# Hybrid attention layer, one core: the first projection pass's weight casts, its two scale-and-shift sums and the late normalisations in another order

## The chip, the cores and the metric

The kernel runs on one core of a Trainium2 chip. The metric is the device time of one execution in microseconds (us). Before the change it is 689.31 us, the median of 3 runs (689.22 to 689.42).

The core has five engines with a queue each: PE (TensorE, matrix products), ACT (ScalarE), DVE (VectorE), POOL (GpSimd) and SP, which here only issues transfers (DMAs). An engine takes its instructions in order, and where one needs another engine's result it waits on a semaphore. PE writes its results to PSUM; ACT and DVE read them there ("evacuate" them).

## What is computed

One residual layer over 1024 rows x 1024 columns, cut to the part that matters here:

```
u = layer_norm(x) * (1 + scale) + shift        # scale, shift = silu(c) @ w_ada + b_ada
h = u @ w_in                                   # q, k, v, g of two groups of 8 heads
y = [forgetting attention | stick-breaking attention] * silu(g)
out = layer_norm(1.19 * x + gate * (y @ w_out)) * ln_g + ln_b
```

Everything is float32 in and out. The products are made at nearly that precision out of two rounded parts: an operand a becomes `hi`, its value rounded to a shorter format, and `lo`, the rounded remainder a - hi. A product then is three: hi x hi, lo x hi and hi x lo. So for every operand somebody has to make a *cast* (hi) and a *remainder* (lo).

## The kernel before: the first pass

The change lies within the first 55 us, the first pass over the projection. It works on rows 0 to 511 (four tiles x_0 to x_3 of 128 rows) and makes five products at once (`ALL`, the names `st_q`, `st_k`, `st_g`, `st_q`, `st_k` in the profile): q, k and g of head pair 0, q and k of pair 1. The width of 1024 is cut into eight blocks, `kb` = 0 to 7, and the loop at L672 takes them one after the other. For block kb+1, while PE multiplies block kb:

- SP loads the weights: `wss` (w_ada's two slices, for scale and shift, `load_ss`, L152), `raws` (the slice of w_in for four of the five products, `load_w4`, L574; one load brings blocks 4 and 5 together, another 6 and 7).
- DVE sums scale and shift out of `wss` (`mod_terms`, L233: two instructions L230 for each block, part 0 and part 1, each followed by a short read-out into `modc`).
- PE transposes the four x tiles' 128 columns into the PSUM tile `xT_early` (`u_turn`, L239, L242). There is one such tile for all blocks from 2 on, so the transposes of a block wait until the last reader of the block before is through.
- ACT makes `uh` of it, the cast of u (L248), and writes the unrounded u back into `xT_early` (L249); together that is `u_round`.
- DVE makes `ul`, the remainder of u, out of both (`u_rest`, L260, L261). It is the last reader of `xT_early`.
- ACT makes the cast of the weights and POOL their remainder (`start_split`, L575 to L599; the names are `whi_stk`/`wlo_stk` for blocks 0 to 2 and `hw` from block 3 on, in pairs of blocks: one `hw` holds 3 and 4, the next 5 and 6, the last 7).

PE's order is written out by hand (`manual_schedule`) and so is SP's. In a block it is: four products with the weights' casts (hi), four with their remainders (lo), the four transposes of block kb+1, the fifth product's two, then the five products with `ul` (`start_steps`, L601). The order of ACT, DVE and POOL is set by a scheduler; `with after(i)` tells it that an instruction goes behind i, and `in_turn` (L223) chains the sums and `ul` among themselves in the order written.

After block 7 the first value tiles follow (`v_first`, L781: rows of v for pairs 0 and 1, `v_tile` L346): tile 0 into one half of the PSUM tile `st_late`, tile 1 into `v`, tile 2 into the other half of `st_late`, tile 3. Each has four evacuations, in turn ACT (L360) and DVE (L361), twice. Then `late_round` (L773) makes u of rows 512 to 1023 in the same way, and for that x_4 to x_7 have to be normalised (`norm_stats` L208, `norm_x` L213): x_4 and x_5 by ACT (L218), x_6 and x_7 by DVE (L217, `NORM_ON`), behind their statistics (L197, L198, L189 on DVE, L191 and L192 on POOL).

At the very start PE is kept busy with products whose result nobody reads (`busy`, L174; `WARM`, L75): four before anything else, one behind the transposes of x_0 and one behind those of x_1 (L639).

Of the kernel before, what the change touches and what calls it, by code (L numbers as in the profile page):

```python
# [8 lines left out]
F32 = mybir.dt.float32  # L9
F32R = mybir.dt.float32r  # L10
AF = mybir.ActivationFunctionType
ALU = mybir.AluOpType

P = 128
SEQ = 1024
D = 1024
NB = 8
# [10 lines left out]
def tile_hybrid_layer(  # L28
# [17 lines left out]
    nc = tc.nc  # L46
# [21 lines left out]
    def t_tile(name):  # L68
        return ps.tile([P, 512], F32, tag="T", bufs=2, name=name)
# [2 lines left out]
        return ps.tile([P, 2, 512], F32, tag="S", bufs=1, name=name)  # L72

    RING = 5
    WARM = (4, 1, 1, 0, 0)  # L75
    NORM_ON = {6: nc.vector, 7: nc.vector}
    FLOG = 4
    FROW = 8
# [4 lines left out]
    def after(*instructions):  # L83
        stack = ExitStack()
        for i in instructions:
            stack.enter_context(tc.issue_after(i.ins))
        return stack


    ident = cp.tile([P, P], F32, tag="ident", name="ident")  # L90
# [80 lines left out]

    def busy(n, acc):  # L174
        for _ in range(n):
            nc.tensor.matmul(acc.rearrange("p (a b) -> p a b", a=4), ident,
                             ident.rearrange("p (a b) -> p a b", a=1).to_broadcast([P, 4, P]),
                             start=True, stop=True)

    busy(WARM[0], sc_all[:, 0, :])  # L180
# [32 lines left out]
    def norm_x(t, a=0, b=D):  # L213
        mv, rs = norm[t]
        xs = xt[t][:, a:b]
        if t in NORM_ON:
            return NORM_ON[t].tensor_scalar(xs, xs, mv[:, 0:1], rs[:, 0:1], op0=ALU.subtract, op1=ALU.mult)  # L217
        return nc.scalar.activation(xs, xs, AF.Identity, scale=rs[:, 0:1], bias=rs[:, 1:2])  # L218
# [14 lines left out]
    def mod_terms(kb, parts=(0, 1)):  # L233
        for i in parts:
            in_turn(mod_part, kb, i)
# [103 lines left out]
    nc.gpsimd.memset(later, 1.0)  # L339
    nc.gpsimd.memset(later[:, :, 0:1], 0.0)  # L340

    def make_v(g):
        for p in (2 * g, 2 * g + 1):
            vt[p] = sb.tile([P, NB, 256], F32R, tag="v", bufs=3, name=f"v_{p}")

    def v_tile(g, t, acc, quarters):  # L346
        n = 264 if g == 1 else 256
        ts_ = slice(t * P, (t + 1) * P)
        for kt in range(NB):
            hi, lo = quarters[kt // 2]  # L350
            s = slice((kt % 2) * n, (kt % 2) * n + n)
            nc.tensor.matmul(acc[:, :n], u_hi[kt][:, ts_], hi[:, s], start=(kt == 0), stop=False)  # L352
            nc.tensor.matmul(acc[:, :n], u_lo[kt][:, ts_], hi[:, s], start=False, stop=False)  # L353
            nc.tensor.matmul(acc[:, :n], u_hi[kt][:, ts_], lo[:, s], start=False, stop=(kt == NB - 1))  # L354
            if kt == 3:
                yield
        for i in range(2):
            v4 = vt[2 * g + i].rearrange("p t (x c) -> p t x c", c=HD)
            a4 = acc[:, i * P:(i + 1) * P].rearrange("p (x c) -> p x c", c=HD)
            nc.scalar.copy(v4[:, t, 0::3, :], a4)  # L360
            nc.vector.tensor_tensor(v4[:, t, 1:3, :], a4, v4.bitcast(F32)[:, t, 0::3, :],  # L361
                                    op=ALU.subtract)
        if g == 1:
            nc.vector.tensor_tensor(fsb[:, :, t], acc[:, 256:264], bf_sb, op=ALU.add)
        yield
# [220 lines left out]
    def start_split(key):  # L586
        if key[0] == "h" or key[1] < 3:
            hi, lo = ring_w("st" + key[0] + str(key[1]))
        else:
            if key[1] == 3:  # L590
                early_w.append(pt_tile("hw_34"))
            elif key[1] == 5:
                early_w.append(pt_tile("hw_56"))
            home = (early_w[-1][:, (key[1] - 3) % 2, :] if key[1] < 7 else big("sg", 2, "hw_7", F32R))
            hi, lo = home[:, :512], home[:, 512:]
        split[key] = hi, lo
        h3, l3 = (t[:, :512].rearrange("p (m c) -> p m c", m=4) for t in (hi, lo))
        split_at[key] = (nc.scalar.copy(h3, raw_w[key]),
                         nc.gpsimd.tensor_tensor(l3, raw_w[key], h3.bitcast(F32), op=ALU.subtract))  # L599
# [36 lines left out]
    for t in range(4):  # L636
        u_turn(0, tp=xt_early, tiles=(t,))
        u_turn(1, tp=acc0[NW], tiles=(t,))
        busy(WARM[1 + t], acc0[NW - 1])  # L639
    start_split(("k", 0))  # L640
    rounded = u_split(0)
    mod_terms(1)
# [29 lines left out]
    for kb in range(NB):  # L672
        last = kb == NB - 1
        if last:
            start_steps(ALL[:2], acc0, kb)
            for n in range(2):
                evac_m(*START[n], 0, acc0[n])
            start_steps(ALL[2:], acc0, kb)
            break
        start_steps(ALL[:4], acc0, kb, parts=(0,))  # L680
        if kb == 0:
            u_turn(2, tp=xt_early)
        elif kb > 1:
            u_turn(kb + 1, tp=xt_early)
        with after(split_at["k", kb + 1][0]):
            rounded = u_split(kb + 1) if kb == 0 else u_round(kb + 1)
        if kb == 0:
            with after(rounded):
                start_split(("h", 0))
            mod_terms(2)  # L690
        else:
            parts = range(2 if kb + 2 < NB else 0)
            mod_terms(kb + 2, parts[:1])
            rest = in_turn(u_rest, kb + 1)
            mod_terms(kb + 2, parts[1:])
        if kb == 0:
            start_steps(ALL[:4], acc0, kb, parts=(1,))
        elif kb == 1:
            start_steps(ALL[:4], acc0, kb, parts=(1,))
            for k in range(2):  # L700
                start_steps(ALL[4:], acc0, k)
        else:
            start_steps(ALL[4:], acc0, kb, parts=(0,))
            start_steps(ALL, acc0, kb, parts=(1,))
        if kb + 2 < NB:
            start_split(("k", kb + 2))
        if kb == 2:
            start_split(("h", 1))
        if kb + 5 < NB:
            load_ss(kb + 5)  # L710
            if kb == 0:
                load_w4(6, 2)
        if kb == 2:
            for n in range(2):
                v0_load(n)
            load_x(4)
            for n in range(2, 4):
                v0_load(n)
            for t in range(5, NB):
                load_x(t)  # L720
        if kb == 5:
            with after(*split_at["k", NB - 1]):
                for n in range(4):
                    v0_split(n)
            norm_stats(4)
            norm_stats(5)
            norm_x(4)
            norm_x(5)
        if kb == 6:
            with after(rest):  # L730
                for t in (6, 7):
                    norm_stats(t)
                    norm_x(t)
            make_v(0)

    wg = {}
# [44 lines left out]
    def v_first(t, acc):  # L781
        for _ in v_tile(0, t, acc, v0_w):
            pass

    v_first(0, late_acc[:, 0, :])
    v_first(1, t_tile("v_0_1"))
    for kt in range(4):
        load_gate(kt)
# [349 lines left out]
```

## Time and profile before

| | before |
|---|---|
| median of 3 runs | 689.31 us |
| the profiled execution | 689.13 us |
| its span, first to last instruction | 687.2 us |
| PE busy in the span | 671.8 us (98%) |
| DVE, POOL, ACT busy | 488.3, 403.2, 381.3 us |
| PE busy between 30 and 40 us, and 50 and 60 us | 9.38 and 9.27 of 10 us |
| moved by DMA, 20 to 42 us | 383 to 442 GB/s in each 2 us |

A row of the timeline gives the start, the duration, the engine, the line of the kernel, the operation, what it writes <- what it reads, the shape, the count, and in brackets how long the engine had been idle and whose end released it. PE's matrix products are pipelined: the duration of one is longer than the distance from its start to the next one's, and it is the distance that counts. "PEld" is the loading of the stationary operand, which overlaps PE's work. A row of the waits reads: who waited <- for whom, us in total, times, the longest.

### The profile page before, as it was taken

What the parts mean: (1) busy time and instruction counts of PE and PEld (TensorE: products, weight loads), DVE (VectorE), ACT (ScalarE), POOL (GpSimd) and SP (SyncE); (2) the same over time, 40 slices, a digit from 0 to 9 for tenths busy, and PEclk for the clock granted to TensorE, in tenths of its full rate; (3) what the DMA queues carried; (4) which work ended last, traced back from release to release, by engine and by line L of the source; (5) the groups of instructions that cost most, each with busy time, mean ns of one, the idle gap of its engine ahead of it and who ended that gap; (6) DMA issues with size and microseconds to landing.
All of it is one profiled execution on the core that took longest, in us unless ns stands there. A gap on an engine that the chain in (4) does not pass through costs nothing.

```text
span 687.2 us, 11196 instructions
## 1 busy us (share of the span) xinstructions
PE 671.8 (98%) x3709; PEld 571.2 (83%) x3709; DVE 488.3 (71%) x996; ACT 381.3 (55%) x857; POOL 403.2 (59%) x529
## 2 busy tenths in 40 slices
PE   8999999999999999999999999999999999999995
PEld 5788888788998888889988888889988878888885
DVE  6696769968668677777776675766676778785645
ACT  6566377756667666566665564655565666521000
POOL 5650179746447655556369878668785365655411
PEclk9999999999999999999999999999999999999998
DMA  9954422112102112112134455254352297143301
GB/s 335 409 221 170 152 74 76 40 26 55 40 9 70 40 54 55 40 50 58 36 104 128 161 162 166 80 176 146 116 163 72 60 353 300 59 174 106 118 31 61
DMA packets 45272, 81.54 MB, mean 119 GB/s; under 512 B 5216, under 2 KB 19360, under 8 KB 44960
## 3 DMA queue, kind: packets, MB, share of 16 engines
q1 hardware_dynamic: 43632, 76.54, 33.8%
q10 hardware_dynamic: 1584, 4.31, 1.9%
q8 instruction: 29, 0.48, 0.3%
q14 instruction: 27, 0.22, 0.1%
HBM read 60.34 MB, written 16.29 MB: 112 GB/s over the span
## 4 chain that ended last, share of the span: by engine, by line
PE 83%; DVE 6%; DMA 4%; ACT 3%; POOL 2%; issue 2%; DVEq 0%; POOLq 0%; ACTq 0%
PE m L296 9%; PE pv L526 9%; PE m L298 9%; PE m L297 9%; PE T L509 9%; PE S L458 4%; PE S L457 4%; PE o L901 4%; PE o L900 4%; PE o L899 4%; PE v L354 3%; PE v L352 3%; PE v L353 3%; DMA wss<-in_w_ss_dram 3%; PE st_late L612 1%
## 5 line engine op out<-in xcount | busy, mean ns | idle before, releaser
L296 PE MATMUL m<-uh,whi 128*128 128x512 f32 x304 | 125.0, 411 | 0.7 <-DVE kl L284 0.7
L512 DVE TENSOR_TENSOR pt<-T,pt 128x512 fp32r<-128x512 f32 (+2 forms) x192 | 103.1, 551 | 26.0 <-ACT pt L511 24.2
L298 PE MATMUL m<-uh,wlo 128*128 128x512 f32 x304 | 119.7, 394 | 0.0
L297 PE MATMUL m<-ul,whi 128*128 128x512 f32 x304 | 119.6, 394 | 0.0
L511 ACT CAST pt<-T 128x512 fp32r<-128x512 f32 (+2 forms) x192 | 88.6, 478 | 42.0 <-PE T L509 39.1
L492 POOL TENSOR_TENSOR be<-be,kp 128x127 f32<-128x127 f32 (+3 forms) x64 | 77.1, 1204 | 37.2 <-DVE kp L490 27.6
L486 DVE TENSOR_TENSOR_SCAN kp<-kp,floor 128x512 f32<-128x512 f32 (+2 forms) x64 | 65.1, 1018 | 27.6 <-ACT kp L479 25.4
L526 PE MATMUL pv<-pt,v 128*128 128x512 f32 x320 | 82.8, 388 | 0.3 <-DVE pt L512 0.3
L536 POOL TENSOR_TENSOR ty<-ty,sg 64x256 f32<-64x256 f32 x64 | 47.0, 734 | 42.6 <-DVE ty L535 18.3
L473 POOL TENSOR_SCALAR a<-a,l 128x1024 f32<-128x1024 f32 (+3 forms) x64 | 48.2, 752 | 39.7 <-DVE l L471 29.5
L298 PEld LDWEIGHTS m<-uh,wlo 128*128 128x128 f32 x304 | 57.1, 188 | 13.7
L457 PE MATMUL S<-k,q 128*128 128x512 f32 (+5 forms) x192 | 66.2, 346 | 0.2 <-DVE nm L465 0.2
L296 PEld LDWEIGHTS m<-uh,whi 128*128 128x128 f32 x304 | 57.2, 188 | 10.1 <-DVE kl L284 1.1
L458 PE MATMUL S<-kl,qz 128*128 128x512 f32 (+5 forms) x192 | 65.3, 341 | 0.0
L470 ACT ACTIVATE a<-a,nm 128x1024 f32<-128x1024 f32 (+3 forms) x64 | 49.8, 778 | 26.4 <-DVE nm L465 25.8
L297 PEld LDWEIGHTS m<-ul,whi 128*128 128x128 f32 x304 | 57.3, 189 | 7.9
L526 PEld LDWEIGHTS pv<-pt,v 128*128 128x128 f32 x320 | 55.4, 189 | 9.6 <-DVE pt L512 0.6
L479 ACT ACTIVATE kp<-S 128x128 f32<-128x128 f32 (+3 forms) x64 | 41.8, 652 | 33.7 <-PE S L458 31.3
L465 DVE CUSTOM_DVE_ANT_0 a<-S,fb 128x1024 f32<-128x1024 f32 (+3 forms) x64 | 48.2, 754 | 15.8 <-PE S L458 12.4
L431 ACT CAST qz<-q 64x128 fp32r<-64x128 f32 x128 | 37.3, 295 | 34.5 <-PE S L458 33.3
L352 PE MATMUL v<-whi_v,uh 128*128 128x256 f32 (+1 forms) x192 | 55.5, 289 | 0.0
L354 PE MATMUL v<-wlo_v,uh 128*128 128x256 f32 (+1 forms) x192 | 54.3, 283 | 0.3 <-POOL wlo_v L127 0.3
(290 smaller groups left out, 1625.0 us busy)
## 6 DMA issues: line engine op xcount, KB each, us to landing
raw<-in_w_qkg_dram SPq DMA_DIRECT2D x38, 256.0 KB, 2.6
wss<-in_w_ss_dram SPq DMA_DIRECT2D x12, 512.0 KB, 8.4
x<-in_x_dram SPq DMA_DIRECT2D x8, 512.0 KB, 6.8
k<-k SPq DMA_DIRECT2D x32, 128.0 KB, 2.3
wg<-in_w_gate_dram SPq DMA_DIRECT2D x8, 512.0 KB, 4.2
raw_o<-in_w_out_dram SPq DMA_DIRECT2D x16, 256.0 KB, 3.0
fb<-f_dr ACTq DMA_DIRECT2D x8, 512.0 KB, 4.2
wo_dr<-whi_o SPq DMA_DIRECT2D x16, 256.0 KB, 2.2
```

Of the source, the lines that this page charges most:

```text
L296: nc.tensor.matmul(acc, hi[:, c], u_hi[kt][:, s], start=(kt == 0), stop=False)
L297: nc.tensor.matmul(acc, hi[:, c], u_lo[kt][:, s], start=False, stop=False)
L298: nc.tensor.matmul(acc, lo[:, c], u_hi[kt][:, s], start=False, stop=(kt == NB - 1))
L352: nc.tensor.matmul(acc[:, :n], u_hi[kt][:, ts_], hi[:, s], start=(kt == 0), stop=False)
L354: nc.tensor.matmul(acc[:, :n], u_hi[kt][:, ts_], lo[:, s], start=False, stop=(kt == NB - 1))
L457: nc.tensor.matmul(S[:, s, :w], qst[p][h][:, qs], kst[p][h][:, ks], start=True, stop=False)
L458: nc.tensor.matmul(S[:, s, :w], z, klo[p][:, ks], start=False, stop=True)
L486: last_dve = nc.vector.tensor_tensor_scan(rv, rv, floor[:, :ke - lo], initial=0.0, op0=ALU.mult, op1=ALU.max)
L492: nc.gpsimd.tensor_tensor(be[:, :ke - 1], be[:, :ke - 1], kp[:, 1:ke], op=ALU.mult)
L511: nc.scalar.copy(hi[:, :n, qo:qo + P], t3)
L512: lows[:] = [nc.vector.tensor_tensor(lo[:, :n, qo:qo + P], t3, hi.bitcast(F32)[:, :n, qo:qo + P], op=ALU.subtract)]
L526: nc.tensor.matmul(acc2[:, :, q0:], vt[p][:, kb, h * P:(h + 1) * P], pt[:, :, q0:], start=(kb == 0), stop=(kb == last))
```

## The change

Four edits, all in the first pass and what follows it directly.

1. Two more `busy` products, of half the width (256 columns), behind the transposes of x_2 and of x_3.
2. The weight splits of blocks 4 to 7 are issued one iteration later, behind `u_round` of the block ahead: 4 and 5 behind `u_round(4)`, 6 behind `u_round(5)`, 7 behind `u_round(6)`.
3. In iterations 3 and 4 `u_rest` goes ahead of both sums of the block after (until now between them).
4. x_5, x_6 and x_7 are normalised behind the four evacuations of value tile 0. x_4 and all statistics stay where they are written.

```diff
-    WARM = (4, 1, 1, 0, 0)
+    WARM = (4, 1, 1, 1, 1)
...
-    def busy(n, acc):
+    def busy(n, acc, m=4):
...
+    v_evacs = []
...
-            nc.scalar.copy(v4[:, t, 0::3, :], a4)
-            nc.vector.tensor_tensor(v4[:, t, 1:3, :], a4, v4.bitcast(F32)[:, t, 0::3, :],
-                                    op=ALU.subtract)
+            v_evacs.append(nc.scalar.copy(v4[:, t, 0::3, :], a4))
+            v_evacs.append(nc.vector.tensor_tensor(v4[:, t, 1:3, :], a4, v4.bitcast(F32)[:, t, 0::3, :],
+                                                   op=ALU.subtract))
...
-        busy(WARM[1 + t], acc0[NW - 1])
+        busy(WARM[1 + t], acc0[NW - 1], 4 if t < 2 else 2)
...
-        with after(split_at["k", kb + 1][0]):
+        with after(*split_at["k", kb + 1][:1] if kb < 2 else ()):
             rounded = u_split(kb + 1) if kb == 0 else u_round(kb + 1)
...
-            mod_terms(kb + 2, parts[:1])
+            late = kb in (3, 4)
+            mod_terms(kb + 2, () if late else parts[:1])
             rest = in_turn(u_rest, kb + 1)
-            mod_terms(kb + 2, parts[1:])
+            mod_terms(kb + 2, parts if late else parts[1:])
...
-        if kb + 2 < NB:
-            start_split(("k", kb + 2))
         if kb == 2:
             start_split(("h", 1))
+        elif kb < 2:
+            start_split(("k", kb + 2))
+        elif kb + 2 < NB:
+            with after(rounded):
+                for k in ((4, 5) if kb == 3 else (kb + 2,)):
+                    start_split(("k", k))
...
             norm_x(4)
-            norm_x(5)
         if kb == 6:
             with after(rest):
                 for t in (6, 7):
                     norm_stats(t)
-                    norm_x(t)
             make_v(0)
...
     v_first(0, late_acc[:, 0, :])
+    with after(*v_evacs):
+        for t in (5, 6, 7):
+            norm_x(t)
```

The scheduler's order changes only within these first 55 us: on PE two rows are added and nothing else moves, on SP nothing moves, and on ACT, DVE and POOL every row behind the first value tiles' evacuations stands where it stood.

ACT in blocks 3 to 6, before. `uh_127` to `uh_130` are blocks 3 to 6, `xT_early` the write-back; the casts are block 4 (`hw_321` from `raws_248`), 5 (`hw_396` from `raws_248`), 6 (`hw_396` from `raws_296`) and 7 (`hw_449`):

```order
L248 ACTIVATE uh_127<-xT_early,modc 128x512
L249 ACTIVATE xT_early<-xT_early,modc 128x512
L598 CAST hw_321<-raws_248 128x512
L248 ACTIVATE uh_128<-xT_early,modc 128x512
L249 ACTIVATE xT_early<-xT_early,modc 128x512
L598 CAST hw_396<-raws_248 128x512
L598 CAST hw_396<-raws_296 128x512
L598 CAST hw_449<-raws_296 128x512
L248 ACTIVATE uh_129<-xT_early,modc 128x512
L249 ACTIVATE xT_early<-xT_early,modc 128x512
L248 ACTIVATE uh_130<-xT_early,modc 128x512
```

The same place after; block 4's cast is now `hw_323`, 5's and 6's `hw_398`, 7's `hw_451`:

```order
L248 ACTIVATE uh_127<-xT_early,modc 128x512
L249 ACTIVATE xT_early<-xT_early,modc 128x512
L248 ACTIVATE uh_128<-xT_early,modc 128x512
L249 ACTIVATE xT_early<-xT_early,modc 128x512
L600 CAST hw_323<-raws_250 128x512
L600 CAST hw_398<-raws_250 128x512
L248 ACTIVATE uh_129<-xT_early,modc 128x512
L249 ACTIVATE xT_early<-xT_early,modc 128x512
L600 CAST hw_398<-raws_298 128x512
L248 ACTIVATE uh_130<-xT_early,modc 128x512
L249 ACTIVATE xT_early<-xT_early,modc 128x512
L600 CAST hw_451<-raws_298 128x512
```

Block 4's cast went from ahead of `uh_128` (block 4) to behind its write-back, and the casts of 6 and 7 each behind one more block's u.

DVE from the remainder of block 3 (`ul_135`) on, before; `wss_245` are the sums of block 4, `wss_293` those of block 5, `ul_136` the remainder of block 4:

```order
L261 TENSOR_TENSOR ul_135<-xT_early,uh_127 128x512
L230 ISA wss_245,modc<-sc_all,wss_245,bss_sb 128x1024
L230 ISA modc 128x1
L230 ISA wss_293,modc<-sc_all,wss_293,bss_sb 128x1024
L230 ISA modc 128x1
L261 TENSOR_TENSOR ul_136<-xT_early,uh_128 128x512
```

And after, where the same tiles are called `wss_247` and `wss_295`:

```order
L261 TENSOR_TENSOR ul_135<-xT_early,uh_127 128x512
L230 ISA wss_247,modc<-sc_all,wss_247,bss_sb 128x1024
L230 ISA modc 128x1
L261 TENSOR_TENSOR ul_136<-xT_early,uh_128 128x512
L230 ISA wss_295,modc<-sc_all,wss_295,bss_sb 128x1024
```

`ul_136` moved ahead of the first sum of the block after; `ul_137` of block 5 moves in the same way ahead of the first sum of block 6.

DVE around the evacuation of value tile 0 (`v_520` and `v_521` out of `st_late`), before, the two L217 being the normalisations of x_6 and x_7:

```order
L271 SCALAR_TENSOR_TENSOR q_1_251<-st_q_148,q_1_251 64x512
L284 TENSOR_TENSOR kl_254<-st_k_149,k_1_253 64x512
L189 BN_AGGR mv_a_514<-st_a_511 128x2
L217 TENSOR_SCALAR x_369<-x_369,mv_a_505,rs_a_507 128x1024
L361 TENSOR_TENSOR v_520<-st_late,v_520 128x128
L217 TENSOR_SCALAR x_369<-x_369,mv_a_514,rs_a_516 128x1024
L361 TENSOR_TENSOR v_521<-st_late,v_521 128x128
```

And after:

```order
L284 TENSOR_TENSOR kl_256<-st_k_149,k_1_255 64x512
L189 BN_AGGR mv_a_506<-st_a_503 128x2
L363 TENSOR_TENSOR v_519<-st_late,v_519 128x128
L189 BN_AGGR mv_a_514<-st_a_511 128x2
L363 TENSOR_TENSOR v_520<-st_late,v_520 128x128
L217 TENSOR_SCALAR x_369<-x_369,mv_a_506,rs_a_508 128x1024
L217 TENSOR_SCALAR x_369<-x_369,mv_a_514,rs_a_516 128x1024
```

Both normalisations now stand behind both evacuations of tile 0; on ACT the normalisation of x_5 went behind its two evacuations in the same way.

More of the change, by code (lines that the diff above doesn't have):

```diff
@@ L170, in tile_hybrid_layer @@
     sc_all = s_tile("sc_all")
-    def busy(n, acc):
+    def busy(n, acc, m=4):
         for _ in range(n):
-            nc.tensor.matmul(acc.rearrange("p (a b) -> p a b", a=4), ident,
-                             ident.rearrange("p (a b) -> p a b", a=1).to_broadcast([P, 4, P]),
+            nc.tensor.matmul(acc.rearrange("p (a b) -> p a b", a=4)[:, :m, :], ident,
+                             ident.rearrange("p (a b) -> p a b", a=1).to_broadcast([P, m, P]),
                              start=True, stop=True)
```

## The prediction

> **What bounds the kernel now.** I read the page's first part, then PE's waits by stretch, then the chain of waits, and for the places it named the timeline engine by engine. The page:
>
> ```profile
> span 687.2 us, 11196 instructions
> PE 671.8 (98%) x3709; PEld 571.2 (83%) x3709; DVE 488.3 (71%) x996; ACT 381.3 (55%) x857; POOL 403.2 (59%) x529
> ```
>
> PE stands still for 15.4 of 687.2 us. Its order is fixed and almost everywhere one product follows the other, so time saved ahead of a place in PE's queue arrives at the end unless a later wait takes it. The question is which of PE's waits lie where the change works. These are the ones of 30 to 80 us, and the largest later one:
>
> ```profile
> PE xT_early L242 <- DVE ul L261: 0.5, 1, 0.5
> PE st_q L612 <- ACT uh L248: 0.4, 1, 0.4
> PE st_late L352 <- DVE v L361: 0.7, 1, 0.7
> PE T L509 <- DVE pt L512: 1.7, 3, 1.4
> ```
>
> Idle time is less than what a wait costs. PE's own rows show it (T stands for the transposes of a block):
>
> ```profile
> 27.19 0.60 PE L242 MATMUL xT_early<-ident,x 128*128 128x128 f32 x4
> 29.76 0.50 PE L612 MATMUL st_q<-uh,hw 128*128 128x512 f32 x1 [0.35 <-ACT uh L248]
> 30.10 0.39 PE L612 MATMUL st_k<-uh,hw 128*128 128x512 f32 x1
> 31.73 0.60 PE L242 MATMUL xT_early<-ident,x 128*128 128x128 f32 x4
> 36.70 0.66 PE L242 MATMUL xT_early<-ident,x 128*128 128x128 f32 x4 [0.52 <-DVE ul L261]
> 40.74 0.60 PE L242 MATMUL xT_early<-ident,x 128*128 128x128 f32 x4
> 42.82 0.39 PE L612 MATMUL st_q<-uh,hw 128*128 128x512 f32 x1
> ```
>
> From 30.10 to 31.73 there are seven products, 0.233 us each. The first product after a wait is followed only 0.34 us later (29.76 to 30.10), so a wait costs 0.11 us beyond its length. An undisturbed block is eight products (1.86 us) from its first product to the next T, and 2.08 us from T to the first product of the next block (40.74 to 42.82). From T of block 4 at 27.19 to 42.82 that makes 2.08 + 3 x (1.86 + 2.08) = 13.90 us; it took 15.63. So blocks 4 to 6 lose 1.73 us. What holds them:
>
> ```profile
> 23.78 10.83 DMA wss<-in_w_ss_dram
> 34.75 1.28 DVE L230 CUSTOM_DVE_ANT_0 wss<-sc_all,wss,bss_sb 128x1024 f32<-128x1024 f32 x1 [2.05 <-DMA wss<-in_w_ss_dram]
> 35.96 0.69 DVE L261 TENSOR_TENSOR ul<-xT_early,uh 128x512 fp32r<-128x512 f32 x1
> 36.56 1.28 DVE L230 CUSTOM_DVE_ANT_0 wss<-sc_all,wss,bss_sb 128x1024 f32<-128x1024 f32 x1
> 37.76 0.08 DVE L230 DVE_READ_ACCUMULATOR2_ANT modc<- 128x1 f32 x1
> ```
>
> The first row is from the chain: block 6's `wss` lands at 34.61. DVE waited 2.05 us for it, and the remainder of block 5 stood behind the sum that waited; PE's T of block 6 waited for that remainder until 36.70. A sum takes 1.21 us to the next instruction, a remainder 0.60.
>
> **Part 1: casts behind u, remainder ahead of the sums.** Here are ACT's rows, POOL's remainder of block 4, the load of PE's weights, and DVE's read-out of block 4's second sum:
>
> ```profile
> 28.41 0.62 ACT L598 CAST hw<-raws 128x512 fp32r<-128x512 f32 x1 [3.08 <-DMA raws<-in_w_qkg_dram]
> 28.93 0.77 ACT L248 ACTIVATE uh<-xT_early,modc 128x512 fp32r<-128x512 f32 x1
> 29.61 0.74 ACT L249 ACTIVATE xT_early<-xT_early,modc 128x512 f32<-128x512 f32 x1
> 30.27 0.62 ACT L598 CAST hw<-raws 128x512 fp32r<-128x512 f32 x1
> 37.94 0.78 ACT L248 ACTIVATE uh<-xT_early,modc 128x512 fp32r<-128x512 f32 x1 [3.28 <-DVE modc L230]
> 29.10 1.28 POOL L599 TENSOR_TENSOR hw<-raws,hw 128x512 fp32r<-128x512 f32 x1 [3.34 <-ACT hw L598]
> 29.76 0.19 PEld L612 LDWEIGHTS st_q<-uh,hw 128*128 128x128 f32 x1 [0.78 <-ACT uh L248]
> 27.57 0.09 DVE L230 DVE_READ_ACCUMULATOR2_ANT modc<- 128x1 f32 x1
> ```
>
> Block 4. The first cast waited 3.08 us for its load, and `uh(4)` stood behind it, though its sums were read out at 27.66 and T had ended at 27.79. Behind T instead, `uh(4)` starts at 27.83, the write-back 0.68 later at 28.51, and block 4's cast 0.66 later at 29.17, ending at 29.79: 0.76 us later than before. PE now waits for the cast and not for `uh`: first product at 29.85 instead of 29.76. POOL's remainder follows the cast by 0.07 us and takes 1.28: it ends at 31.15, and the fifth product, due at 30.89, waits until 31.20. With the 0.11 us of a restart T of block 5 comes at 31.20 + 0.34 + 3 x 0.233 = 32.24, against 31.73. **The edit loses 0.51 us here.**
>
> Blocks 5 to 7. ACT is free by then, so `uh(5)` starts right after T at 32.24 + 0.64 = 32.88 (0.60 us of T and 0.04 to the reader), write-back 33.56 to 34.30. DVE, no longer behind the sum, makes the remainder at 34.33; PE comes to T of block 6 undisturbed at 32.24 + 3.94 = 36.18, against 36.70, and by then the remainder is done (35.02). The sums of block 6 start at 34.93, behind the landing at 34.61 by 0.3 us, and are read out at 37.35 instead of 37.76; `uh(6)` follows by 0.18 us (37.76 to 37.94) at 37.53. It ends at 38.31, PE starts block 6 at 38.37, T of block 7 at 38.37 + 0.34 + 7 x 0.233 = 40.34, against 40.74. The first sum of block 7 starts at 37.35, and its `wss` has landed by then: issued at 27.69, it took
>
> ```profile
> 27.69 0.33 SPq L155 DMA_DIRECT2D wss<-in_w_ss_dram  x1
> DMA to landing us min/median/max: 9.4/9.4/9.4
> ```
>
> 9.4 us, so 37.1. The casts of 6 and 7 go behind the write-backs of 5 and 6 (34.2 and 38.9); with 0.62 and 1.28 us their remainders end at 36.2 and 40.9, ahead of use at about 39.4 and 43.3, so they cost nothing. **Sum of this part: 0.40 us faster at block 7.** Its bounds are 0.51 slower, if nothing is won back after block 4, and 1.73 faster, all that blocks 4 to 6 lose. I take 0.40 since each step has its row.
>
> A rule of the skill speaks against the edit at block 4. The Trainium skill, TensorE: Matmul & The Clock Gate, section "Step-by-step: what each phase is for", says that PE pulls the loading of weights ahead of running products. By it a wait for `uh` leaves the weights loaded, while a wait for the weights themselves exposes their load. The row speaks against it here: block 4's weights were cast by 29.03, PE's load waited all the same and started with the product at 29.76. So I price both kinds of wait at the same 0.11 us; by the rule the two new waits would each show 0.19 us of load instead.
>
> **Part 2: late normalisations behind the evacuation.** DVE and ACT, then PE:
>
> ```profile
> 50.31 0.76 DVE L217 TENSOR_SCALAR x<-x,mv_a,rs_a 128x1024 f32<-128x1024 f32 x1
> 51.11 0.29 DVE L361 TENSOR_TENSOR v<-st_late,v 128x128 fp32r<-128x128 f32 x1
> 51.83 0.81 DVE L217 TENSOR_SCALAR x<-x,mv_a,rs_a 128x1024 f32<-128x1024 f32 x1 [0.43 <-POOL rs_a L192]
> 52.55 0.29 DVE L361 TENSOR_TENSOR v<-st_late,v 128x128 fp32r<-128x128 f32 x1
> 51.89 0.28 PE L354 MATMUL v<-v_w,uh 128*128 128x256 f32 x1
> 52.90 0.39 PE L352 MATMUL st_late<-v_home,uh 128*128 128x256 f32 x1 [0.73 <-DVE v L361]
> 53.12 0.28 PE L353 MATMUL st_late<-v_home,ul 128*128 128x256 f32 x1
> 55.86 1.03 PE L242 MATMUL xT<-ident,x 128*128 128x128 f32 x8
> ```
>
> PE's value tile 2 writes into `st_late` and waits for the last evacuation of tile 0, which stands behind both normalisations. These products come every 0.12 us, so the tile was due at 52.01 with its second product at 52.13; that came at 53.12. The wait costs 0.99 us. Without x_6's normalisation ahead, DVE's first evacuation comes 0.80 us earlier, at 50.31; one ACT cast (0.27) and two hand-overs later the second, 50.66 to 50.95. That is a microsecond before PE asks, and both ends move with part 1. The wait goes altogether: **0.99 us faster**, bounds 0 and 0.99.
>
> What is late next: x_5 on ACT and x_6, x_7 on DVE. Their readers are the late transposes, at 55.86 before, now at 54.47. x_6 takes DVE from 51.0 to 51.7 and x_7, which POOL's scale released at 51.83, from there to 52.6 even without the shift of part 1: 1.9 us of room.
>
> **Part 3: two more fillers.**
>
> ```profile
> 10.65 1.02 PE L176 MATMUL st_q<-ident 128*128 128x512 f32 x2
> 12.14 0.33 PE L242 MATMUL xT_early<-ident,x 128*128 128x128 f32 x1 [0.24 <-ACT x L218]
> 13.46 0.50 PE L612 MATMUL st_q<-uh,whi_stk 128*128 128x512 f32 x1 [0.89 <-ACT uh L255]
> ```
>
> Half the columns take half of 1.02 us, 0.5. The first falls into the stretch up to 12.14 in which PE waits for x_3, the second into that up to 13.46; a few hundredths by which T of x_3 might slip are covered by ACT, whose `uh` of block 0 ends only at about 13.4. Cost nothing, bounds 0 and 0.1 (0.24 of cover against 0.5, less the tail of the last transposes). Nor can it gain: PE waits for `uh` with or without it.
>
> **The sum.** 0.40 + 0.99 = 1.39 us. Behind 57 us no instruction moves, so I let all of it through. The profiled execution took 689.13 us, 0.18 under the median; against the median the forecast is 689.31 - 1.39 = **687.9 us**. A measurement can tell 0.2% (1.38 us) from no change, so faster begins below 687.93: the forecast stands on that line.
>
> **The rivals.**
>
> A. *Waits for weights are dearer than waits for u.* In block 4 both the cast and the remainder are then exposed with their full load: 2 x 0.19 us more, passed on through `ul` and the sums of block 6, takes part 1 to nothing: 688.3 us. For it is that the remainder is the last of its chain (cast 29.79, remainder 31.15); against it the load row at 29.76. It is the mechanism of the skill's rule above. A worse form, in which block 4's 0.51 us is not won back at all, gives 689.31 - 0.99 + 0.51 = 688.8.
>
> B. *More comes back.* PE's wait of 1.4 us for `pt` comes while DVE is behind; a DVE that is relieved earlier might shorten it by up to that: 687.9 - 1.4 = 686.5. Against it: DVE's order there is the same and its work is released by PE.
>
> C. *The gain is given back:* a later wait grows by what PE arrives early, 689.3 us. It needs a transfer or an engine that doesn't move with PE; between 57 us and the end I see no such wait of that size.
>
> D. *Slower: the late normalisations become PE's wait.* If x_7 were done later than 54.47, PE would stand at the late transposes; beyond 55.86 the kernel is slower than before, at 57.24 by 0.2% (690.7 us). For it: x_7's scale goes over DVE, POOL and DVE again. Against it: 1.9 us of room, where 4.7 are needed.
>
> **How the numbers follow.** The forecast (both parts, within some 0.4 us) has 0.64: 0.37 beyond the line, since in the new order fewer of PE's steps hang on a load's landing, and 0.27 short of it. A has 0.18 (same), B 0.11 (faster), C 0.03 (same), D 0.04 (slower). That makes 0.48 faster, 0.48 the same, 0.04 slower. The range runs from 687.2 (half of B) to 688.8 (the worse form of A).
>
> **What would show it.** Right: no wait of `xT_early` for `ul` and none of `st_late` for `v`; instead, at 29 to 32 us, one of `st_q` for ACT's `hw` and one of the fifth product for POOL's `hw`; T of block 7 at about 40.3, the late transposes at 54.5. Wrong: a PE wait at the late transposes, block 4's lost half microsecond still there at block 7, or a stretch behind 60 us whose PE idle time grew.

## The result and the profile after

| | before | after |
|---|---|---|
| median | 689.22 us (11 runs, 688.92 to 689.44) | 687.57 us (11 runs, 687.36 to 687.82) |
| the profiled execution | 689.13 us | 687.36 us |
| its span | 687.2 us | 685.6 us |
| T of block 4, T of block 7, late transposes start | 27.19, 40.74, 55.86 | 27.13, 40.26, 54.35 |
| late transposes to the end of the span | 631.34 us | 631.25 us |

T stands for the transposes of a block, as in the prediction. The ratio is 0.9977, with a 95% interval of 0.9968 to 0.9986: 1.65 us, or 0.24%, faster. Measured twice more beside other kernels, the same change gave 0.9981 (0.9972 to 0.9990) and 0.9979 (0.9971 to 0.9988): 1.42 and 1.39 us.

The page's first part, after:

```profile
span 685.6 us, 11206 instructions
PE 671.9 (98%) x3713; PEld 571.4 (83%) x3713; DVE 488.1 (71%) x996; ACT 381.5 (56%) x857; POOL 403.3 (59%) x529
```

PE is as busy as before (671.9 against 671.8 us) in a span that is 1.6 us shorter, so the difference is time in which PE stood still. Which of its stops went, and which came, the waits tell; the first two rows are all of those between 30 and 80 us, the third the largest later one:

```profile
PE st_q L614 <- ACT hw L600: 0.4, 1, 0.4
PE st_q L614 <- POOL hw L601: 0.2, 1, 0.2
PE T L511 <- DVE pt L514: 1.8, 3, 1.4
```

The waits of `xT_early` for `ul`, of `st_q` for `uh` and of `st_late` for `v` are gone. The view of before has a fourth row for this stretch, which the prediction's list left out: 0.2 us of `st_g0b` (at 60.80) for DVE's `sg`. It is not listed any more after the change; it lies behind the late transposes, where the two kernels differ by 0.09 us in all, so it carries no more than that. Two short waits came, one for the cast and one for the remainder of block 4's weights. PE's rows show where:

```profile
27.13 0.60 PE L242 MATMUL xT_early<-ident,x 128*128 128x128 f32 x4
...
29.77 0.50 PE L614 MATMUL st_q<-uh,hw 128*128 128x512 f32 x1 [0.42 <-ACT hw L600]
30.10 0.39 PE L614 MATMUL st_k<-uh,hw 128*128 128x512 f32 x1
...
31.14 0.50 PE L614 MATMUL st_q<-uh,hw 128*128 128x512 f32 x1 [0.17 <-POOL hw L601]
31.48 0.39 PE L614 MATMUL st_k<-uh,hw 128*128 128x512 f32 x1
...
32.17 0.60 PE L242 MATMUL xT_early<-ident,x 128*128 128x128 f32 x4
...
36.12 0.60 PE L242 MATMUL xT_early<-ident,x 128*128 128x128 f32 x4
...
40.26 0.60 PE L242 MATMUL xT_early<-ident,x 128*128 128x128 f32 x4
```

Block 4 comes out 0.44 us later than before (32.17 against 31.73), block 5 0.58 us earlier (36.12 against 36.70), block 6 0.48 us earlier (40.26 against 40.74). DVE's two rows say why the sign turns: the remainder of block 5 now stands ahead of the sum of block 6, and by the time the remainder is made the sum's load is there, so that neither waits for a load to land:

```profile
34.26 0.69 DVE L261 TENSOR_TENSOR ul<-xT_early,uh 128x512 fp32r<-128x512 f32 x1 [1.95 <-ACT xT_early L249]
34.87 1.27 DVE L230 CUSTOM_DVE_ANT_0 wss<-sc_all,wss,bss_sb 128x1024 f32<-128x1024 f32 x1
```

At the value tiles, DVE's evacuations of tile 0 now come first and the normalisations behind them; PE's tile 2 starts at 51.50, 0.12 us behind the product ahead of it, which is the usual distance there:

```profile
50.05 0.29 DVE L363 TENSOR_TENSOR v<-st_late,v 128x128 fp32r<-128x128 f32 x1
50.68 0.29 DVE L363 TENSOR_TENSOR v<-st_late,v 128x128 fp32r<-128x128 f32 x1 [0.21 <-ACT v L362]
51.01 0.81 DVE L217 TENSOR_SCALAR x<-x,mv_a,rs_a 128x1024 f32<-128x1024 f32 x1
52.27 0.81 DVE L217 TENSOR_SCALAR x<-x,mv_a,rs_a 128x1024 f32<-128x1024 f32 x1 [0.45 <-POOL rs_a L192]
```

```profile
51.38 0.28 PE L356 MATMUL v<-v_w,uh 128*128 128x256 f32 x1
51.50 0.28 PE L354 MATMUL st_late<-v_home,uh 128*128 128x256 f32 x1
54.35 1.04 PE L242 MATMUL xT<-ident,x 128*128 128x128 f32 x8
```

The last row is the late transposes. From there to the end both kernels take the same time within 0.1 us: what was gained ahead of them arrived at the end.

### The profile page after: what moved, and what is told of

It is laid out like the page before. It is cut to its first block, busy times and chain, and to the rows that moved or that the text cites. A ratio compares the mean times of both kernels' runs of the same rounds, so it can differ in the third digit from the quotient of the medians.

```text
span 685.6 us, 11206 instructions
## 1 busy us (share of the span) xinstructions
PE 671.9 (98%) x3713; PEld 571.4 (83%) x3713; DVE 488.1 (71%) x996; ACT 381.5 (56%) x857; POOL 403.3 (59%) x529
## 4 chain that ended last, share of the span: by engine, by line
PE 85%; DVE 6%; ACT 3%; POOL 2%; issue 2%; DMA 1%; DVEq 0%; POOLq 0%; ACTq 0%
PE pv L528 9%; PE m L296 9%; PE m L298 9%; PE m L297 9%; PE T L511 8%; PE o L909 4%; PE o L908 4%; PE o L907 4%; PE S L460 4%; PE S L459 4%; PE v L356 4%; PE v L354 4%; PE v L355 3%; PE st_q L614 1%; PE st_late L614 1%
```

## The experiments

The theory was the prediction's: the normalisations were worth 0.99 us by themselves, casts and remainder together 0.4 us, the two parts add, and the fillers cost nothing. The rivals were that one part carries all of it, and that one of the two moved steps of part 1 does the work alone. The later runs came out of what the first four left open: what limits part 1, and whether the fillers are free. Each group of kernels ran on one chip with its own runs of the kernel before. T4 to T7 in the table is the time from the transposes of block 4 to those of block 7 in the profiled execution; the last column is from T of block 7 to the late transposes. The last three columns come from one execution each, in us like the medians.

| kernel | median (runs) | before | ratio, 95% interval | T of block 4 | T4 to T7 | T7 to late transposes |
|---|---|---|---|---|---|---|
| before | 689.22 (11) | | | 27.19 | 13.55 | 15.12 |
| after | 687.57 (11) | 689.22 | 0.9977, 0.9968 to 0.9986 | 27.13 | 13.13 | 14.09 |
| norms | 688.36 (11) | 689.42 | 0.9986, 0.9977 to 0.9995 | 27.95 | 12.95 | 14.11 |
| no_casts | 688.65 (11) | 689.42 | 0.9991, 0.9982 to 1.0000 | 27.32 | 13.65 | 14.10 |
| no_rest | 688.37 (11) | 689.42 | 0.9984, 0.9975 to 0.9993 | 27.35 | 13.27 | 14.13 |
| no_norms | 688.19 (11) | 689.42 | 0.9984, 0.9975 to 0.9992 | 27.60 | 13.10 | 14.12 |
| after_again | 688.12 (11) | 689.54 | 0.9981, 0.9972 to 0.9990 | 27.31 | 13.13 | 14.09 |
| nofill | 687.75 (9) | 689.54 | 0.9977, 0.9967 to 0.9986 | 27.75 | 13.13 | 14.09 |
| mid | 688.22 (11) | 689.54 | 0.9981, 0.9973 to 0.9990 | 27.71 | 13.23 | 14.11 |
| best | 687.58 (7) | 689.54 | 0.9973, 0.9962 to 0.9983 | 27.65 | 12.53 | 14.10 |
| after_third | 688.07 (11) | 689.46 | 0.9979, 0.9971 to 0.9988 | 27.31 | 13.10 | 14.11 |
| nofill_again | 687.91 (11) | 689.46 | 0.9976, 0.9967 to 0.9985 | 27.56 | 13.11 | 14.13 |
| best_again | 687.52 (8) | 689.46 | 0.9971, 0.9961 to 0.9982 | 27.73 | 12.52 | 14.10 |
| best_nofill | 687.10 (5) | 689.46 | 0.9968, 0.9955 to 0.9980 | 27.72 | 12.54 | 14.12 |

One thing has to be known to read it. T of block 4 lies between 27.13 and 27.95 in these profiles, and it need not go by the kernel: `mid`, whose rows are the change's in the same order up to block 4, has 27.71, the change itself 27.13 and twice 27.31. The first loads land at different times. In the kernel `norms`, for one, DVE waited 0.97 us for x_2:

```profile
8.10 0.69 DVE L197 BATCH_NORM_STATS2 st_a<-x 128x6 f32<-128x512 f32 x1 [0.97 <-DMA x<-in_x_dram]
```

In the six profiles in which DVE waited 0.45 us or more for x_2, T of block 4 comes at 27.56 to 27.95, in the other eight at 27.13 to 27.65; what else moves it was not looked into. So stretches are compared from T of block 4 on, and spans of single profiles are not.

**norms: the normalisations alone.** The kernel before with edit 4 only (`v_evacs` is filled as in the change):

```diff
-            norm_x(5)
...
-                    norm_x(t)
...
+    with after(*v_evacs):
+        for t in (5, 6, 7):
+            norm_x(t)
```

> The kernel before with the fourth edit alone (x_5 to x_7 normalised behind value tile 0's evacuations; the scheduler moves three rows for it and nothing else). Theory: PE loses 0.99 us at value tile 2 before and nothing in this kernel, while block 7 starts at 42.8 us as before; the late transposes start at 54.87 instead of 55.86 and the time is 0.99 us lower, 688.2 against 689.2. Rival 1, the value tile's wait is the whole gain of the change and the first pass gives nothing: 1.65 us lower, 687.6. Rival 2, PE's wait only moves to the late transposes: they start at 55.8 and the time is 689.2.

Measured: 688.36 against 689.42 us, 1.06 us faster. PE's wait for `v` is gone, and T of block 7 to the late transposes takes 14.11 instead of 15.12 us: 1.01 us, the theory's 0.99. Its blocks 4 to 7 hold a lesson of their own, in PE's and DVE's rows:

```profile
27.95 0.60 PE L242 MATMUL xT_early<-ident,x 128*128 128x128 f32 x4
...
36.86 0.66 PE L242 MATMUL xT_early<-ident,x 128*128 128x128 f32 x4 [0.49 <-DVE ul L261]
40.90 0.60 PE L242 MATMUL xT_early<-ident,x 128*128 128x128 f32 x4
```

```profile
34.90 1.28 DVE L230 CUSTOM_DVE_ANT_0 wss<-sc_all,wss,bss_sb 128x1024 f32<-128x1024 f32 x1 [2.05 <-DMA wss<-in_w_ss_dram]
36.11 0.69 DVE L261 TENSOR_TENSOR ul<-xT_early,uh 128x512 fp32r<-128x512 f32 x1
```

Block 4 began 0.76 us later than in the kernel before (27.95 against 27.19), the sum of block 6 only 0.15 us later (34.90 against 34.75), and T of block 7 0.16 us later. In the old order these blocks hang on the landing of block 6's load and not on PE. In the new order T of block 7 follows T of block 4 by 13.10 to 13.13 us, in six profiles with T of block 4 anywhere from 27.13 to 27.75. So what part 1 gains depends on the start: 0.48 us with T of block 4 at 27.13 (40.26 against 40.74), next to nothing at 27.75, where the new order's kernel `nofill` below had T of block 7 at 40.88 (here the old order had 40.90). At the start of `norms` itself the new order would lose: 27.95 + 13.1 is 41.05, an estimate, against the 40.90 that the old order had.

**no_casts: the change without edit 2.** The remainder goes ahead of both sums, but the weights' casts stay ahead of `uh`:

```diff
-        with after(*split_at["k", kb + 1][:1] if kb < 2 else ()):
+        with after(split_at["k", kb + 1][0]):
...
+        if kb + 2 < NB:
+            start_split(("k", kb + 2))
         if kb == 2:
             start_split(("h", 1))
-        elif kb < 2:
-            start_split(("k", kb + 2))
-        elif kb + 2 < NB:
-            with after(rounded):
-                for k in ((4, 5) if kb == 3 else (kb + 2,)):
-                    start_split(("k", k))
```

> The changed kernel without its second edit: weight casts in the order of before, the remainders of blocks 4 and 5 still ahead of both sums. Theory: the two edits need each other. Block 4's cast waits for its load again, u of block 4 starts at about 28.9, its write-back ends at 30.35, and as the remainder now goes first, the sums of block 5 start at 31.0 instead of 29.6, those of block 6 at 35.6 instead of 34.75. Block 7 starts at 43.1, 0.3 us later than before and 0.8 later than in the changed kernel; time 688.4 (0.8 above the changed kernel). Rival, each edit gives its own share: the remainder alone gives about half of the part's 0.4 to 0.5 us, block 7 at 42.6, time 687.8.

Measured: 688.65 us, 0.29 above `norms`, with overlapping intervals. The profile shows how part 1's gain is lost. The cast still holds `uh` and its write-back, and now the sums stand behind the remainder that needs the write-back:

```profile
30.34 0.69 DVE L261 TENSOR_TENSOR ul<-xT_early,uh 128x512 fp32r<-128x512 f32 x1 [2.55 <-ACT xT_early L249]
30.94 1.27 DVE L230 CUSTOM_DVE_ANT_0 wss<-sc_all,wss,bss_sb 128x1024 f32<-128x1024 f32 x1
...
35.59 1.28 DVE L230 CUSTOM_DVE_ANT_0 wss<-sc_all,wss,bss_sb 128x1024 f32<-128x1024 f32 x1
```

The first sum of block 6 starts at 35.59 instead of 34.87, and PE waits for `uh` in blocks 5 and 6 (idle 0.43 and 0.45 us). T4 to T7 is 13.65 us, no better than the 13.55 of the kernel before. Edit 3 without edit 2 brings nothing.

**no_rest: the change without edit 3.** The casts go behind `uh`, the remainder stays between the sums:

```diff
-            late = kb in (3, 4)
+            late = False
```

> The changed kernel without its third edit: casts behind u as in the change, but the remainder between the two sums as before. Theory: the transposes of block 5 come late at 32.2 as in the changed kernel, u of block 5 comes early at 32.8, but the remainder of block 5 waits behind a sum that waits for its load until 34.75, so the transposes of block 6 come at 36.7 and block 7 at 42.8, both as before: the casts alone are worth 0 us, time 688.05 (0.5 above the changed kernel). Rival, each edit gives its own share: block 7 at 42.6, time 687.8. Rival, the lost half microsecond of block 4 stays: block 7 at 43.3, time 688.5.

Measured: 688.37 us, the same as `norms` (688.36). DVE waits for the landing with the remainder behind it, as in the kernel before:

```profile
34.64 1.28 DVE L230 CUSTOM_DVE_ANT_0 wss<-sc_all,wss,bss_sb 128x1024 f32<-128x1024 f32 x1 [2.04 <-DMA wss<-in_w_ss_dram]
35.85 0.69 DVE L261 TENSOR_TENSOR ul<-xT_early,uh 128x512 fp32r<-128x512 f32 x1
```

T of block 6 follows at 36.59 and T of block 7 at 40.62. So each edit alone is worth nothing that the medians show, and the profiles show that only the pair lets PE's blocks go by PE and not by the landing. What the pair is worth the medians of this group do not settle either, as the next run shows.

**no_norms: the change without edit 4.** The text of edit 4 is undone, and the scheduler is left free:

```diff
+            norm_x(5)
...
+                    norm_x(t)
...
-    with after(*v_evacs):
-        for t in (5, 6, 7):
-            norm_x(t)
```

> The changed kernel without its fourth edit: nothing in the program holds the late normalisations back. The scheduler nevertheless leaves both of DVE's behind value tile 0's evacuations, now that the rows ahead have moved; only ACT's normalisation of x_5 goes ahead of them. Theory: the order counts and not the edit. ACT is through with x_5 at about 49.8, the second evacuation ends at about 51.0, PE wants the tile at 51.5: no wait, late transposes at 54.35, time as the changed kernel (687.6, within 0.2). Rival, the edit itself is needed: PE waits 0.99 us as before, late transposes at 55.3, time 688.6.

Measured: 688.19 us, and T of block 7 to the late transposes 14.12 us: as expected, the wait did not come back. DVE's rows show that the scheduler, with casts and remainders in the new places, put both DVE normalisations behind tile 0's evacuations by itself; only x_5 on ACT went ahead of them:

```profile
50.59 0.29 DVE L363 TENSOR_TENSOR v<-st_late,v 128x128 fp32r<-128x128 f32 x1
51.21 0.29 DVE L363 TENSOR_TENSOR v<-st_late,v 128x128 fp32r<-128x128 f32 x1 [0.33 <-ACT v L362]
51.52 1.70 DVE L217 TENSOR_SCALAR x<-x,mv_a,rs_a 128x1024 f32<-128x1024 f32 x2
```

The order on DVE stayed, so the run says that part 2's microsecond belongs to an order and not to an edit: edit 4 forces it, and on top of edits 2 and 3 it is not needed. By its time this kernel is then the change once more, 1.23 us below the kernel before. Expected were the 1.65 us of the change's first measurement. Beside `norms`, which has part 2 without part 1, it is the one place where the pair of part 1 can be read from medians of one group: 688.19 against 688.36, 0.17 us, with overlapping intervals. Even that is not the pair alone, since `norms` has no fillers and this kernel has them (so have `no_casts` and `no_rest`); medians without fillers come out lower below. So the 0.4 us of part 1 rests on the profiles, and on executions that begin as early as those of before and after.

**after_again, nofill, mid, best.** The first four left the size of part 1 open: the change still has T4 to T7 at 13.13 us, where undisturbed blocks would take 3 x 3.94 = 11.82 us. The next group looked for the rest. `after_again` is the change itself.

> The changed kernel once more, on the chip of the three below. Theory and rival alike: 1.65 us below the kernel before, 0.9976, give or take what the start of the span brings (the transposes of block 4 came at 27.1 to 28.0 us in the profiles so far, with nothing of the change ahead of them); from the transposes of block 4 to those of block 7 13.1 us, against 13.55 before; no wait at value tile 2.

Measured: 688.12 against 689.54 us, 1.42 us faster.

`nofill` takes edit 1 out:

```diff
-    WARM = (4, 1, 1, 1, 1)
+    WARM = (4, 1, 1, 0, 0)
```

> The changed kernel without the two fillers. Theory: PE waits for x_3 and for u of block 0 with or without them; the first product of block 0 starts in the same 0.1 us behind the end of its u, the products behind it come every 0.23 us as before, time as the changed kernel within 0.1 us. Rival, the fillers keep PE's clock up through that gap: without them products behind 13.5 us come slower than 0.23 us, and the time rises by 0.5 us or more. Rival, the fillers hold up the transposes of x_3: without them the first product of block 0 starts 0.1 to 0.2 us earlier.

Measured: 687.75 us, 0.37 below `after_again`, with overlapping intervals. More on it below.

`mid` puts block 4's cast between `uh` and the write-back of block 4, so that PE gets its weights 0.7 us earlier:

```diff
-        nc.scalar.activation(u_hi[kb][:, a:b], full, AF.Identity, scale=modc[:, kb, 0:1], bias=modc[:, kb, 1:2])
+        first = nc.scalar.activation(u_hi[kb][:, a:b], full, AF.Identity, scale=modc[:, kb, 0:1], bias=modc[:, kb, 1:2])
+        if (kb, a) == (4, 0):
+            with after(first):
+                start_split(("k", 4))
+            with after(split_at["k", 4][0]):
+                return nc.scalar.activation(full, full, AF.Identity, scale=modc[:, kb, 0:1], bias=modc[:, kb, 1:2])
...
-                for k in ((4, 5) if kb == 3 else (kb + 2,)):
+                for k in (kb + 2,):
```

> The changed kernel with block 4's weight cast moved between u of block 4 and its write-back (one pair of ACT rows changes places, nothing else). Theory: the half microsecond that PE loses in block 4 is that of the cast behind the write-back. The cast ends 0.66 us earlier, PE's wait for it goes, the fifth product still waits 0.35 us for POOL, the transposes of block 5 come 0.6 us earlier (4.4 instead of 5.04 us behind those of block 4); but then the sums of block 6 wait for their load, which lands at 34.6 us, so block 7 starts only 0.1 us earlier: time 0.1 below the changed kernel. Rival, the block 4 loss goes through to the end: 0.6 us below it.

Measured: 688.22 us, no gain over `after_again` (688.12). Block 4 went as expected: T of block 5 comes 4.37 us behind T of block 4, against 5.04 in the change. But nothing of the 0.67 us reaches block 7 (T4 to T7 13.23 us). The theory at that point was that the landing of block 6's load bounds those blocks, and it was wrong: DVE does not wait for it here. ACT's and DVE's rows show what bounds them:

```profile
29.53 0.75 ACT L253 ACTIVATE xT_early<-xT_early,modc 128x512 f32<-128x512 f32 x1
...
33.51 0.78 ACT L248 ACTIVATE uh<-xT_early,modc 128x512 fp32r<-128x512 f32 x1 [2.69 <-DVE modc L230]
```

```profile
30.32 0.69 DVE L266 TENSOR_TENSOR ul<-xT_early,uh 128x512 fp32r<-128x512 f32 x1 [2.23 <-ACT xT_early L253]
30.92 1.27 DVE L230 CUSTOM_DVE_ANT_0 wss<-sc_all,wss,bss_sb 128x1024 f32<-128x1024 f32 x1
```

The cast moved the write-back 0.5 us back, the remainder of block 4 waits for the write-back, the sums of block 5 stand behind the remainder, and `uh` of block 5 waits for the sums (the 2.69 us in brackets) although its transposes were done at 32.7. The same chain holds `uh` of block 6 (it waited 2.69 us for its sums, too), and there PE stands:

```profile
38.98 0.50 PE L619 MATMUL st_q<-uh,hw 128*128 128x512 f32 x1 [0.46 <-ACT uh L248]
```

PE's gain at block 4 was paid back one engine further on.

`best` is `mid` with three more edits: the loads of `wss` of blocks 6 and 7 are issued in halves, the remainder of block 5 goes back between the two sums of block 6, which arrive one by one now, and x_4 is normalised late too:

```diff
-        for a in ((0, 1), (1, 2)) if kb < 6 else ((0, 2),):
+        for a in ((0, 1), (1, 2)) if kb < 8 else ((0, 2),):
...
-            late = kb in (3, 4)
+            late = kb == 3
...
-            norm_x(4)
...
-        for t in (5, 6, 7):
+        for t in (4, 5, 6, 7):
```

> The kernel above and three more steps: the loads for the sums of blocks 6 and 7 in two halves each, as blocks 0 to 5 have them; the remainder of block 5 between the two sums of block 6 again (that of block 4 stays ahead of both); x_4 normalised behind value tile 0 like the others. Theory: behind block 4 the first pass hangs on the landing of block 6's load alone; with its first half there a microsecond earlier, the transposes of block 6 come 8.4 us behind those of block 4 (9.0 in the changed kernel), those of block 7 12.2 us behind them (13.1), no wait at value tile 2, time 0.9 below the changed kernel. Rival, the second half lands when the whole did, so the second sum and block 7 gain at most 0.2 us.

Measured: 687.58 us, 0.54 below `after_again` on the same chip. T4 to T7 is 12.53 us, 0.60 less than in the change; about two thirds of what was expected. PE and DVE:

```profile
27.65 0.60 PE L242 MATMUL xT_early<-ident,x 128*128 128x128 f32 x4
...
40.18 0.60 PE L242 MATMUL xT_early<-ident,x 128*128 128x128 f32 x4
```

```profile
33.90 1.28 DVE L230 CUSTOM_DVE_ANT_0 wss<-sc_all,wss,bss_sb 128x1024 f32<-128x1024 f32 x1 [0.54 <-DMA wss<-in_w_ss_dram]
```

The first half lands at about 33.9, ahead of the 34.87 at which the change started that sum, and DVE waits only 0.54 us for it. The halved loads and the place of the remainder were not tried one by one; the late x_4 shows no gain (T of block 7 to the late transposes 14.10 us, as in the other kernels of the new order). With this kernel T of block 7 stands where the change has it (40.18 against 40.26) although block 4 began half a microsecond later.

**after_third, nofill_again, best_again, best_nofill.** The last group repeats the three kernels that lie close together and joins the last two edits.

> The changed kernel, for the three below: 0.998 of the kernel before, from the transposes of block 4 to those of block 7 13.1 us.

> The changed kernel without the two fillers, once more, since the first comparison left 0.4 us between them in favour of no fillers, with the start of the span apart by as much for another reason (the landing of x_2). Theory: fillers cost and bring nothing, the medians lie within 0.2 us of each other. Rival, they cost: again 0.3 us or more below the kernel with them.

> The kernel with the cast of block 4 ahead of the write-back and halved loads, once more. Theory: 12.5 us from the transposes of block 4 to those of block 7 against 13.1, so 0.5 to 0.6 us below the changed kernel again, 0.9973 of the kernel before.

> The same without the two fillers. Theory: as the kernel with them, within 0.2 us. Rival, fillers cost: 0.3 us or more below it, as the first comparison of the changed kernel had it.

Measured: 688.07, 687.91, 687.52 and 687.10 us. `best` is 0.55 us below the change a second time, with T4 to T7 at 12.52 us. Both times the intervals overlap with the change's; two like differences and a stretch that is 0.6 us shorter in the profile speak for it. `best_nofill` has the lowest median of all, 2.36 us below the kernel before (ratio 0.9968, 0.9955 to 0.9980).

The fillers: without them the median was lower each of three times, by 0.37, 0.16 and 0.42 us. The expectations had allowed 0.1 and twice 0.2 us. The profiles show no reason. In the stretch they are put in, PE waits for `uh` of block 0 with and without them; here is the first product and the next transposes of the change, and of `nofill`:

```profile
13.58 0.50 PE L614 MATMUL st_q<-uh,whi_stk 128*128 128x512 f32 x1 [0.53 <-ACT uh L255]
...
15.53 0.60 PE L242 MATMUL xT_early<-ident,x 128*128 128x128 f32 x4
```

```profile
14.19 0.50 PE L614 MATMUL st_q<-uh,whi_stk 128*128 128x512 f32 x1 [1.15 <-ACT uh L255]
...
16.15 0.60 PE L242 MATMUL xT_early<-ident,x 128*128 128x128 f32 x4
```

The wait is longer without them (1.15 against 0.53 us), but in both the first product starts 0.05 us behind the end of `uh`, so the fillers hold nothing up there. From the first product to the transposes it is 1.95 and 1.96 us, so the products behind the gap are no slower without them, as they would be if the fillers had kept PE's clock up (granted clock 0.997 with them, 0.998 without). The start at 14.19 instead of 13.58 is that execution's landing of x_2, 0.45 us late on DVE. Each pair's intervals overlap, so whether the fillers cost some tenths, and by what, stays open.

## Why the prediction was right

The forecast was 687.9 us: 1.39 us, read from one profiled execution, off the median of the runs shown, 689.31. The change came out at 687.57, 688.12 and 688.07 us, 1.65, 1.42 and 1.39 us below the kernel before beside it. It stood on its own line of 0.2%, and the result lies there: 0.24%, 0.21% and 0.20%.

**Block 4 loses half a microsecond: right.** First product 29.77 (29.85 predicted), fifth 31.14 (31.20), T of block 5 32.17 (32.24). The constant 0.06 to 0.08 is the start of this execution: T of block 4 was at 27.13 instead of 27.19.

**Blocks 5 and 6 win it back with 0.4 on top: right for this start.** T of block 6 at 36.12 (36.18), T of block 7 at 40.26 (40.34). From T4 to T7 the gain is 13.55 - 13.13 = 0.42 us. What the step did not say is that it compares two orders that hang on different events, the old one on a landing and the new one on PE; 0.40 holds for a block 4 that begins at 27.2. That the execution before the change and the one after it both began there (27.19 and 27.13) is luck: `norms` began at 27.95, where the term would be a small loss, and in that group the medians show 0.17 us for it, fillers included. With `no_casts` and `no_rest` each part of it alone gave nothing, so the pair was rightly priced as one term.

**The normalisations 0.99 us: right.** `norms` alone gave 1.06 us by the medians and 1.01 by the profile; in the change it is 1.03 (15.12 - 14.09). The late transposes came at 54.35 (54.47 predicted).

**What is late next: right in kind, off in size.** x_7 was expected ready at 52.6 and was ready at 53.08 (52.27 + 0.81), because POOL's scale took longer beside DVE's normalisation (last section). Of the 1.9 us of room 1.3 us were left.

**Fillers at nothing:** the profile agrees; the medians lean towards a cost of some tenths and do not settle it.

**The rivals.** A, dearer waits for weights, is refuted by rows: behind the wait for the cast the next product came 0.33 us later (29.77 to 30.10), behind that for the remainder 0.34 (31.14 to 31.48), and behind that for `uh` it was 0.34 before. The load of the weights stands in the same place all three times. It starts with the waiting product, at 29.76 before and so here:

```profile
29.77 0.19 PEld L614 LDWEIGHTS st_q<-uh,hw 128*128 128x128 f32 x1 [0.85 <-ACT hw L600]
31.14 0.19 PEld L614 LDWEIGHTS st_q<-uh,hw 128*128 128x128 f32 x1 [0.61 <-POOL hw L601]
```

So neither kind of wait had its weights loaded ahead, and both cost the same. By the prediction's reading of the Trainium skill, TensorE: Matmul & The Clock Gate, "Step-by-step: what each phase is for", where PE pulls loads ahead of running products, only the two waits for weights would have shown the load; the rows do not bear this out. B didn't come: the wait for `pt` is 1.4 us still. C didn't: the late transposes to the end took 631.34 and 631.25 us. D didn't: no wait at the late transposes.

What remains is a tenth or two between the profile's 1.51 us at the late transposes and the medians' 1.39 to 1.65. The medians of one and the same kernel scatter by as much (the kernel before: 689.22 to 689.54), and no cause is sought for it.

## What to carry to other kernels

Where an in-order engine waits for a landing, look at what stands behind the waiting instruction: here moving a 0.6 us remainder ahead of it was worth nothing until its own input, held back by a cast on another engine, came earlier too, so such moves are to be priced and tried as pairs. A step moved ahead of PE's next need is paid for by whoever stood behind it (`mid` gave PE 0.67 us and took it back through write-back, remainder and sums), so follow the chain at least to the second block. And compare stretches from a common event, not from the start of the span, when the first loads land at scattered times; where an old order hangs on a landing and a new one on an engine, look at more than one start before giving the gain a size.

## What the runs showed of the hardware

A POOL instruction of 128 x 1 takes longer when it starts while DVE runs a normalisation of 128 x 1024. The change's rows:

```profile
50.41 0.57 POOL L192 TENSOR_TENSOR rs_a<-rs_a,mhalf 128x1 f32<-128x1 f32 x1
...
51.25 0.98 POOL L192 TENSOR_TENSOR rs_a<-rs_a,mhalf 128x1 f32<-128x1 f32 x1
```

The second runs beside DVE's normalisation of 51.01 to 51.82 and takes 0.98 us instead of 0.57; it ends 0.4 us behind DVE. Five more profiles of the same order have 0.98 or 0.99 us in this place (`after_again`, `after_third`, `nofill`, `nofill_again`, `mid`). Beside DVE's statistics, sums and remainders of q and k the same instruction keeps its 0.56 or 0.57 us, and so it does in `norms`, where it starts 0.4 us ahead of DVE's normalisation. That agrees with the Trainium skill, SBUF — State Buffer, section "SBUF: two separate sides", by which DVE, in some of its instructions, and GpSimd compete for a pair of ports that whichever starts first holds for its whole instruction; that the normalisation is an instruction of that kind no row here shows. Here it delayed x_7 by 0.4 us with PE not waiting; on a path without room it would count.

The other is the start: T of block 4 moved by up to 0.8 us between executions (27.13 to 27.95), half of what this change is worth in all, and it was 27.56 or later in all six in which DVE waited 0.45 us or more for x_2 to land.
